# Three PSUM tiles of a decoder trunk draw their banks under another tag

## The chip, the cores and the metric

The kernel runs on one core of a Trainium2 chip. The metric is the device time of one execution in microseconds (us). TensorE (PE in the profile) does the matmuls, VectorE (DVE) and ScalarE (ACT) the elementwise work, GpSimd (POOL) a few small operations, and SP issues the DMAs. Every engine works through its own instructions in the order in which the built program holds them. A matmul writes into PSUM, which this kernel uses as eight banks of 128 x 512 fp32.

## The reference, cut to what is computed

Two layers over 256 tokens of width 1024. Each layer is a half-step FFN, a token mixer, a second half-step FFN and a gated embedding, each closed by a layer norm. The token mixer is where the change lies:

```python
def token_mixing(x, ...):
    h = (x @ w_in).astype(jnp.float32)                # one wide projection
    h_rw, h_gla, h_gdn, h_gate = _split(h, GROUP_SPLITS)
    o_rw = rwkv7_time_mix(h_rw, ...)                  # RWKV-7 recurrence
    o_gla = gla_mix(*_split(h_gla, GLA_SPLITS), ...)  # gated linear attention
    o_gdn = gated_deltanet_mix(*_split(h_gdn, GDN_SPLITS), ...)
    branches = jnp.stack([o_rw, o_gla, o_gdn], axis=2)
    proj = jnp.einsum('btnc,ncd->btnd', branches, w_branch)
    gates = jax.nn.sigmoid(h_gate).reshape(B, T, N_BRANCH, D_MODEL)
    return jnp.sum(gates * proj, axis=2) @ w_o

def gated_deltanet_mix(...):                          # "DeltaNet" below
    q = _l2norm(_heads(q, H, GDN_DK)) * GDN_DK ** -0.5
    k = _l2norm(_heads(k, H, GDN_DK))
    ...
    t_inv = lax.linalg.triangular_solve(eye + lower, ...)   # an inverse per chunk
    ...                                               # then a recurrence over chunks
```

## The kernel before, in words

**Precision.** Every large product is made of three fp32r matmuls: a weight arrives by DMA as `raw` (128 x 1024, one half of a unit), ACT casts it to `hi`, DVE subtracts to get `lo`, and PE runs `hi` with the high part of x (`xh`), `hi` with its low part (`xl`), and `lo` with `xh`.

**Four threads.** Inside a layer's mixer, four Python generators run side by side. S, the stream, makes the blocks of the wide projection: `col_block` fills one PSUM bank, named `cb`, with 48 matmuls of 128 x 256, from two weight halves; then DVE and ACT read the bank (`conv`: one ACT operation and three DVE operations for each 256 columns; `put`: one ACT copy and a DMA to DRAM). R is RWKV (`rwkv`), D is DeltaNet (`gdn`), L is GLA (`gla`). The string `ORDER` says whose next step is recorded. The recorded order is not yet the order on the engines: a scheduler then lists each engine's instructions by priority, and a tile whose pool has no free slot waits for one. So a different pool slot can move instructions on all engines.

**PSUM.** `ps(name, tag)` hands out banks under three tags: A has four banks, F two, G two. `TAGS` overrides the tag by the tile's name. F is what the stream's `cb` blocks rotate through: one bank fills while the other is read out. G is used by the three chains beside it, among others by `lg` (the 64 x 64 products of GLA's eight levels, which take both G banks at once and give them back after a masked copy on DVE), by `rih` and `gih` (the products of the two inverses), `pk`, `gk`, `gks`, `pg` and the transposes `tp`. The rest draws from A.

**The three tiles.** `un` in `unit_norms` is one 128 x 512 matmul that sums squares for the norm of DeltaNet's k and q, four in a layer, each read by an ACT logarithm into `usq`. `ktr` in `gdn` is four transposes in one bank, three times in a layer, read by one ACT copy. `lc` in `gla` is GLA's cross product, two banks in a layer, read by an ACT copy into `lcross`.

**Names in the rows of the mixer.** `rix`, `rih` are RWKV's inverse; `rp`, `ru`, `ry`, `rd` are the matmuls of one of RWKV's four chunk steps, `rpr` and `uz` the copies between them; `pg`, `rv` its output. `pk`, `pq` are DeltaNet's products of k and q; `gig`, `gigt`, `giab` its inverse on DVE; `gix`, `gih`, `gtt`, `gtf`, `gto` its inverse on PE; `gv`, `gd`, `gks`, `go` its recurrence, `gvn`, `gvd`, `grt` the DVE operations between them. `lw` and `latt` are GLA's level weights and its attention, `lo` on PE its output (on DVE, `lo<-raw,hi` is the weight split). `mo`, `var`, `rs` belong to the norm at the end of DeltaNet and GLA. `pj` is the product of a branch with its weights; the first of them needs RWKV's result `bh`, and ends the part in which the threads run side by side.

Of the kernel before, what the change touches and what calls it, by code (L numbers as in the profile page):

```python
# [23 lines left out]
AX = mybir.AxisListType  # L24

RAW, HL, N4, LEAD, FIN = 4, 4, 25, (3, 3), 1
TAGS = {"ab": "A", "gcol": "A", "gih": "G", "gks": "G", "ktr": "F", "lc": "F", "lo": "A", "misc": "G", "pa": "G", "pg": "G", "pj0": "A", "pj1": "A", "pq": "A", "pw": "G", "rih": "G", "st0": "A", "st1": "G", "un": "F"}
PJ = 0
MG = (4, 5)
MO = (3, 3)  # L30
# [204 lines left out]
class Trunk:  # L235
# [66 lines left out]
    def ps(self, name, tag="A"):  # L302

        tag = TAGS.get(name, tag)
        return self.pp.tile([P, 512], F32, tag=tag, name=name, bufs={"A": 4, "F": 2, "G": 2}[tag])
# [1358 lines left out]
```

## Time and profile before

| | us |
|---|---|
| median of 3 runs | 1574.25 (1574.13 to 1577.86) |
| profiled execution, device time | 1568.71 |
| its span, first to last instruction | 1566.9 |
| mean granted TensorE clock | 0.981 |
| mixer of layer 0, first `cb` to first `pj` | 217.0 to 501.4 |
| mixer of layer 1, first `pj` | 1280.3 |

The time of the profiled execution is 1.8 us more than its span, and 5.5 us less than the median. In the profile's tables a row of the view by stages has a stretch of the span, its length, and for each engine the busy time with the count of its instructions; "PEclk" is the clock granted to TensorE as a share of the full one. In the timeline a row has the start, the duration, the engine, the operation with its tiles, the count, and in brackets the idle time of the engine before it and what ended that. In rows of groups the figures behind the bar are the busy time, the mean of one instruction in ns, and the idle time before.

### The profile page before, as it was taken

The numbers are of one execution on the slowest core, as the hardware profiler recorded it, in microseconds if no ns is written. First come the engines' busy times: TensorE is split into PE (matmuls) and PEld (weight loads), VectorE is DVE, ScalarE is ACT, GpSimd is POOL, SyncE is SP. The second block draws the span as 40 slices with busy tenths as digits, with TensorE's granted clock in tenths as the row PEclk, the third lists the DMA queues.
The fourth block names the chain that finished last, engine by engine and source line by source line (L and its number), as shares of the span: only waits on it lengthen the run. The fifth ranks groups of instructions, "written<-read, shape, count | busy, mean of one in ns | idle before, by whom it ended". The sixth has DMA issues, their size and how long they took to land. (4 is left out here: it accounts for less than half of the span.)

```text
span 1566.9 us, 27601 instructions
## 1 busy us (share of the span) xinstructions
PE 1494.9 (95%) x11280; PEld 1356.7 (87%) x11280; DVE 1058.5 (68%) x1597; ACT 873.3 (56%) x1229; POOL 49.1 (3%) x85
## 2 busy tenths in 40 slices
PE   8999999988998999999999999998989889999997
PEld 7999889887987989998789997897979879899986
DVE  5555757787975875556865557577789658745567
ACT  5544558856654554445654445587665555644453
POOL 0000000000002000000000000000000020000001
PEclk9999999989999999999999999999999999999999
DMA  7765655532424655656555666554425256656562
GB/s 257 264 215 189 216 190 161 169 127 80 151 84 168 233 184 177 223 189 216 177 180 192 216 189 194 195 170 153 136 75 156 82 200 219 188 170 222 189 217 81
DMA packets 79775, 277.96 MB, mean 177 GB/s; under 512 B 9376, under 2 KB 9760, under 8 KB 79648
## 3 DMA queue, kind: packets, MB, share of 16 engines
q1 hardware_dynamic: 75744, 262.76, 51.8%
q0 software_dynamic: 3616, 13.11, 2.2%
q8 instruction: 88, 1.44, 0.4%
q10 hardware_dynamic: 288, 0.33, 0.1%
q14 instruction: 39, 0.32, 0.1%
HBM read 264.63 MB, written 11.53 MB: 176 GB/s over the span
## 5 line engine op out<-in xcount | busy, mean ns | idle before, releaser
L223 DVE TENSOR_TENSOR lo<-raw,hi 128x1024 fp32r<-128x1024 f32 (+1 forms) x459 | 555.4, 1220 | 316.1 <-ACT hi L223 313.7
L223 ACT CAST hi<-raw 128x1024 fp32r<-128x1024 f32 (+1 forms) x459 | 474.9, 1047 | 430.1 <-PE h L223 144.1
L223 PE MATMUL h<-xh,hi 128*128 128x256 f32 x1088 | 306.2, 282 | 5.9 <-ACT hi L223 5.5
L223 PE MATMUL h<-xl,hi 128*128 128x256 f32 x1088 | 305.8, 281 | 0.8 <-DVE xl L223 0.8
L223 PE MATMUL h<-xh,lo 128*128 128x256 f32 x1088 | 305.4, 281 | 0.0
L223 PE MATMUL cb<-xh,hi 128*128 128x256 f32 x864 | 247.1, 286 | 14.4 <-DVE c L223 11.1
L223 PE MATMUL cb<-xl,hi 128*128 128x256 f32 x864 | 244.5, 283 | 0.0
L223 PE MATMUL cb<-xh,lo 128*128 128x256 f32 x864 | 243.4, 282 | 0.0
L223 PEld LDWEIGHTS h<-xh,hi 128*128 128x128 f32 x1088 | 204.9, 189 | 7.3 <-ACT hi L223 5.5
L223 PEld LDWEIGHTS h<-xh,lo 128*128 128x128 f32 x1088 | 208.6, 192 | 0.1
L223 PEld LDWEIGHTS h<-xl,hi 128*128 128x128 f32 x1088 | 205.1, 189 | 2.2 <-DVE xl L223 1.0
L223 PEld LDWEIGHTS cb<-xh,hi 128*128 128x128 f32 x864 | 164.7, 191 | 18.8 <-DVE c L223 11.3
L223 PEld LDWEIGHTS cb<-xl,hi 128*128 128x128 f32 x864 | 164.8, 191 | 2.4 <-issue 1.0
L223 PEld LDWEIGHTS cb<-xh,lo 128*128 128x128 f32 x864 | 164.7, 191 | 1.9 <-issue 1.0
L223 PE MATMUL y<-hi,gh 128*128 128x512 f32 x352 | 137.8, 391 | 0.0
L223 PE MATMUL y<-lo,gh 128*128 128x512 f32 x352 | 137.1, 389 | 0.0
L223 PE MATMUL y<-hi,gl 128*128 128x512 f32 x352 | 136.2, 390 | 0.3 <-DVE gl L223 0.3
L223 PE MATMUL tb<-hi,xl 128*128 128x512 f32 x224 | 87.6, 391 | 2.1 <-DVE xl L223 2.1
L223 PE MATMUL tb<-hi,xh 128*128 128x512 f32 x224 | 88.5, 395 | 0.0
L223 PE MATMUL tb<-lo,xh 128*128 128x512 f32 x224 | 88.0, 393 | 0.0
L223 PEld LDWEIGHTS y<-hi,gl 128*128 128x128 f32 x352 | 66.1, 188 | 14.7 <-DVE gl L223 0.8
L223 PEld LDWEIGHTS y<-lo,gh 128*128 128x128 f32 x352 | 66.1, 188 | 12.2
(354 smaller groups left out, 2264.0 us busy)
## 6 DMA issues: line engine op xcount, KB each, us to landing
raw<-in_ws_dram SPq DMA_DIRECT2D x457, 512.0 KB, 4.4
gb<-in_ln_dram SPq DMA_DIRECT2D x16, 512.0 KB, 6.1
gd<-sg SPq DMA_DIRECT2D x32, 256.0 KB, 4.2
sgate<-gd POOLq DMA_DIRECT2D x12, 512.0 KB, 5.8
xd<-x POOLq DMA_DIRECT2D x4, 512.0 KB, 5.8
x<-xd POOLq DMA_DIRECT2D x4, 512.0 KB, 9.0
sw<-in_sw_dram SPq DMA_DIRECT2D x2, 768.0 KB, 8.7
xt<-in_xt_dram SPq DMA_DIRECT2D x4, 256.0 KB, 5.4
```

Of the source, the lines that this page charges most:

```text
L223: ins = f(*args, **kw)
```

## The change

Three entries of the table go from F to G. No instruction is added or removed, and no operation changes; the stream's two banks now serve only the stream, and the two banks of G serve nine more tiles in each layer.

```diff
-TAGS = {"ab": "A", "gcol": "A", "gih": "G", "gks": "G", "ktr": "F", "lc": "F", "lo": "A", "misc": "G", "pa": "G", "pg": "G", "pj0": "A", "pj1": "A", "pq": "A", "pw": "G", "rih": "G", "st0": "A", "st1": "G", "un": "F"}
+TAGS = {"ab": "A", "gcol": "A", "gih": "G", "gks": "G", "ktr": "G", "lc": "G", "lo": "A", "misc": "G", "pa": "G", "pg": "G", "pj0": "A", "pj1": "A", "pq": "A", "pw": "G", "rih": "G", "st0": "A", "st1": "G", "un": "G"}
```

The functions that use the three names:

```python
# unit_norms (DeltaNet's norms)
for sq in sqs:
    for q in range(2):
        ps = self.ps("un", "G")
        self.mm(ps, self.one.to_broadcast([P, P]), sq[:, s])
        nc.scalar.activation(sq[:, s], ps, AF.Ln, bias=self.l2eps)
# gdn
for src, dst in ((kT[:, 0], kt), (v[:, 0], vt[:, 0]), (v[:, 1], vt[:, 1])):
    ps = self.ps("ktr")
    ...
    A.copy(dst, ps.rearrange("p (h c) -> p h c", c=P))
# gla
pss = [self.ps("lc", "G") for _ in range(2)]
```

The scheduler answers with another order. The first place is the norm sums on PE in layer 0, just behind the stream's block that completes DeltaNet's q. Before, on PE:

```order
L223 MATMUL rih<-ritt,riof 64x64 x16
L223 MATMUL rih<-ric,riof 64x64 x16
L223 MATMUL vm<-kc,c_3145 128x128 x3
L223 MATMUL un<-usq,eps 128x512
L223 MATMUL vm<-kc,c_3145 128x128 x5
L223 MATMUL bon<-c_2363,kc 128x512
L223 MATMUL rih<-ric,riof 64x64 x10
L223 MATMUL un<-usq,eps 128x512
L223 MATMUL rih<-ric,riof 64x64 x38
L223 MATMUL un<-usq,eps 128x512 x2
L223 MATMUL pk<-c_2651 128x128 x4
```

Now, on PE at the same place:

```order
L223 MATMUL cb<-xh,lo 128x256
L223 MATMUL un<-usq,eps 128x512 x2
L223 MATMUL vm<-kc,c_3145 128x128 x8
L223 MATMUL bon<-c_2363,kc 128x512
L223 MATMUL cb<-xh,hi 128x256
L223 MATMUL cb<-xl,hi 128x256
```

The two sums for k now come first and together; 82 stream matmuls follow; then come the two sums for q, 20 more stream matmuls, and only then the rest of RWKV's inverse (`rih`), `pq` and `pk`. In all, 102 stream matmuls now stand between `un` and the next `rih`, where none stood.

The second place is DeltaNet's recurrence on PE, late in the mixer. Before, `gd` and `go` stand between blocks of the stream:

```order
L223 MATMUL cb<-xl,hi 128x256
L223 MATMUL cb<-xh,lo 128x256
L223 MATMUL lg<-lw 128x64 x2
L223 MATMUL gd<-gvd,ktst 128x128 x4
L223 MATMUL go<-gvn,dd 128x128 x4
L223 MATMUL lg<-lw 128x64 x6
L223 MATMUL cb<-xh,hi 128x256
```

Now the same instructions on PE follow each other directly:

```order
L223 MATMUL lg<-lw 128x64 x8
L223 MATMUL ry<-ls_2959,vs_3940 64x64
L223 MATMUL lg<-lw 128x64 x4
L223 MATMUL ry<-ls_2961,vs_3940 64x64
L223 MATMUL lg<-lw 128x64 x4
L223 MATMUL ktr<-kc,c_2651 128x128 x4
L223 MATMUL ktr<-kc,c_4418 128x128 x8
L223 MATMUL gv<-vt,giof 128x128 x4
L223 MATMUL lg<-lw 128x64 x8
L223 MATMUL gd<-gvd,ktst 128x128 x4
L223 MATMUL go<-gvn,dd 128x128 x4
```

Of the 1,296 `cb` matmuls of a layer, 1,062 stood ahead of `gix` before and 1,273 stand ahead of it now; behind `gix` 234 were left, and 23 are left now.

The third place is the end of DeltaNet's inverse on DVE, just ahead of `gix`. Now:

```order
L223 TENSOR_TENSOR gigt<-giab 128x225
L223 TENSOR_TENSOR lo<-raw,hi 128x1024
L223 TENSOR_REDUCE giab<-gigt 128x15
L223 TENSOR_TENSOR lo<-raw,hi 128x1024
L223 TENSOR_TENSOR gig<-giab,kc 128x512
L223 STREAM_TRANSPOSE gigt<-gig 128x512
L223 TENSOR_TENSOR gig<-giab,kc 128x512
L223 TENSOR_TENSOR lo<-raw,hi 128x1024
L223 STREAM_TRANSPOSE gigt<-gig 128x512
L223 TENSOR_TENSOR lo<-raw,hi 128x1024 x2
```

From the first copy `rpr<-rp` of RWKV's recurrence to the second of these transposes, DVE held 8 weight splits `lo<-raw,hi` before and holds 13 now, and the 12 `conv` operations of DeltaNet's v (`c_4418`), which were behind the transposes, now stand ahead of them.

## The prediction

> **What bounds the kernel now.** The page comes first: it says which engine sets the time.
>
> ```profile
> span 1566.9 us, 27601 instructions
> PE 1494.9 (95%) x11280; PEld 1356.7 (87%) x11280; DVE 1058.5 (68%) x1597; ACT 873.3 (56%) x1229; POOL 49.1 (3%) x85
> ```
>
> PE is busy for 95% of the span, and the change neither adds nor removes PE work. So only PE's idle time, and the time in which it runs at a lower granted clock, can change. Next comes the view by stages, on the part of layer 0's mixer whose order the change moves: from the `cb` block that completes DeltaNet's q (357.4) over the first `rp` (386.2) and `gix` (418.7) to the first `pj` (501.4); below it the same stages of layer 1.
>
> ```profile
> core 0: us, PE busy (x) PEld busy (x) DVE busy (x) ACT busy (x) POOL busy (x), PEclk, DMA share, GB/s
> 357.40:386.20 28.80, 24.78 (x271) 19.84 (x270) 22.07 (x40) 18.31 (x24) 1.35 (x4) 0.88 0.13 43
> 386.20:418.70 32.50, 32.50 (x337) 30.03 (x336) 30.78 (x68) 20.90 (x31) 0.00 (x0) 1.00 0.52 164
> 418.70:450.00 31.30, 27.58 (x403) 24.39 (x403) 23.94 (x55) 20.28 (x34) 0.52 (x1) 0.89 0.21 68
> 450.00:501.40 51.40, 44.63 (x446) 41.74 (x444) 33.71 (x67) 24.99 (x35) 6.79 (x10) 0.99 0.41 134
> ...
> 1138.10:1165.70 27.60, 23.58 (x271) 18.64 (x270) 21.39 (x39) 18.29 (x24) 1.35 (x4) 0.94 0.13 42
> 1165.70:1198.20 32.50, 32.50 (x337) 30.03 (x336) 31.08 (x69) 20.84 (x31) 0.00 (x0) 1.00 0.52 162
> 1198.20:1229.00 30.80, 26.45 (x404) 23.31 (x404) 24.24 (x55) 20.39 (x34) 0.52 (x1) 0.94 0.23 71
> 1229.00:1280.30 51.30, 44.55 (x445) 41.66 (x444) 33.51 (x67) 24.98 (x35) 5.91 (x8) 0.98 0.41 134
> ```
>
> I call them stages 1 to 4. PE's idle time in layer 0 is 4.02, 0, 3.72 and 6.77, together 14.5. The clock takes 0.12 x 28.8 + 0.11 x 31.3 + 0.01 x 51.4 = 7.4 more. So 144.0 us hold 122.1 of work at full clock and **21.9 of loss**; in layer 1 the same sum gives 15.1 idle and 4.5 of clock, 19.6. Whatever the change does here is the new loss against these two numbers. Who ends the idle time is told by the view of waits for PE in these stages:
>
> ```profile
> PE pj L223 <- ACT bh L223: 6.0, 1, 6.0
> PE un L223 <- ACT usq L223: 4.0, 1, 4.0
> PE gtf L223 <- ACT gt L223: 1.9, 1, 1.9
> PE rv L223 <- ACT rsq L223: 0.8, 1, 0.8
> PE gtt L223 <- DVE giof L223: 0.5, 1, 0.5
> ```
>
> Stage 4 is the one to look at: DeltaNet's recurrence, the last levels of GLA and two RWKV steps run there one behind the other, each waiting for DVE or ACT between two matmuls, and yet PE idles only 0.76 before `rv` and 6.0 before `pj`. What fills the rest is `cb` alone, as the same view restricted to that tile shows:
>
> ```profile
> 386.20:418.70 32.50, 25.34 (x199) 23.34 (x198) 0.00 (x0) 2.84 (x5) 1.00 0.52 164
> 418.70:450.00 31.30, 6.16 (x49) 5.73 (x49) 5.72 (x12) 1.42 (x3) 0.89 0.21 68
> 450.00:501.40 51.40, 23.50 (x188) 21.97 (x186) 0.00 (x0) 2.37 (x4) 0.99 0.41 134
> ```
>
> **Stage 1: the norm sums.** Before, the third `un` stops PE, because ACT, in order, has two table loads, a Silu, an Exp and a square ahead of it.
>
> ```profile
> 371.40 1.22 PE L223 MATMUL un<-usq,eps 128*128 128x512 f32 x1 [4.02 <-ACT usq L223]
> ...
> 366.98 1.06 ACT L223 ACTIVATE c<-c 128x1024 f32<-128x1024 f32 x1
> 368.06 1.28 ACT L223 ACT_TABLE_LOAD   x1
> 369.35 1.06 ACT L223 ACTIVATE usq<-usq 128x1024 f32<-128x1024 f32 x1
> 370.31 1.04 ACT L223 ACTIVATE usq<-c 128x1024 f32<-128x1024 f32 x1
> ```
>
> Now 82 `cb` matmuls stand in that gap. They need weights: the next two halves are cast at 356.1 and 357.4 and last for 48 matmuls, but the casts for the second 48 stand behind ACT's Silu of q, which waits for DVE's last `conv`, and that for the Exp of k ahead of it on DVE. Walking down the new order with these durations, I get: `un` from 357.4, `vm`, `bon`, 48 `cb` to 368.4; Silu 368.3, first cast done 370.4, its `lo` on DVE 371.6. So PE idles some 3.0 (with two matmuls between) before the remaining 34, and about 1.7 more where q's Ln and Exp hold the next casts. The first `rp` then ends near 392.0 instead of 386.9, with 63 more `cb` done. A `cb` matmul goes every 0.12 us (25.34 for 199, less the overlap of their ends), so those are worth 7.5. **Net 2.4 less in a layer.** Bounds: 7.5 less, if no cast is late and the clock stays up (4.02 + 3.46); 1 more, if these waits lower the clock as the old one did.
>
> **Stage 2: the fill runs ahead.** 346 `cb` now stand between there and `gix`, 41.5 of PE; `gk`, `ru`, `ry`, `rd`, `lg` and the rest of the stage are 9 (32.5 less 198 x 0.12). PE needs 50.5. But DVE held 30.78 in 32.50 here. It now gets 5 more `lo`, 12 `conv`, one more pair of `latt`, and the start of the inverse (`at`, `dd`, `gig`, 7.0 between 379.96 and 387.6, since `pk` comes later):
>
> ```profile
> L223 DVE TENSOR_TENSOR lo<-raw,hi 128x1024 fp32r<-128x1024 f32 x457 | 554.1, 1222 | 315.9 <-ACT hi L223 313.4 <-issue 0.3 <-PE cb L223 0.3
> L223 DVE SCALAR_TENSOR_TENSOR c<-cb,cv,c 128x255 f32<-128x255 f32 x48 | 22.6, 477 | 4.1 <-ACT c L223 3.7
> L223 DVE COPY_PREDICATED latt<-masks,lg 128x256 f32<-128x256 uint8 x28 | 13.1, 526 | 4.4 <-PE lg L223 4.4
> ...
> 379.96 1.13 DVE L223 SCALAR_TENSOR_TENSOR at<-pk,nb,dd 128x128 f32<-128x128 f32 x4 [0.42 <-PE pk L223]
> 387.53 0.68 DVE L223 TENSOR_TENSOR c<-c,erke 128x512 f32<-128x512 f32 x1
> ```
>
> 30.8 + 5 x 1.22 + 12 x 0.48 + 2 x 0.53 + 7.0 = 50.7: DVE and PE are now equally long, and each block of 48 needs its second `lo` after only 12 matmuls. The walk finds PE waiting for `lo` four times: 1.3 and 2.8 where the start of GLA's levels stands before it on DVE, 2.0 behind an `lg` group, 1.2 at the inverse's end. **7 more in a layer**, bounds 0 (DVE runs ahead, as it did) and 12 (DVE starts as late as its 6.7 of idle time in stage 1 allow, on top of half of that in order waits). `gix` then starts near 450 where its 211 extra `cb` and one `lg` group (25.3 + 1.1) would put it at 445: 5 behind, stages 1 and 2 together.
>
> **Stages 3 and 4: the uncovered tail.** 82.7 before, less these 26.4 that are done already: even at 56.3. PE's work there at full clock is 82.7 - 10.5 - 4.0 - 26.4 = 41.8 (10.5 idle and 4.0 of clock, from the stages above). Walking the new order from `gix` = 0 with the rows' durations:
>
> ```profile
> 438.78 1.09 PE L223 MATMUL gtt<-kc,giof 128*128 128x128 f32 x8 [0.52 <-DVE giof L223]
> 441.81 0.45 PE L223 MATMUL gtf<-gt,at 128*64 128x64 f32 x8 [1.93 <-ACT gt L223]
> 501.41 0.79 PE L223 MATMUL pj<-bh,hi 128*128 128x256 f32 x2 [6.02 <-ACT bh L223]
> ...
> 458.39 1.23 DVE L223 TENSOR_TENSOR dgate<-dgate,br 128x1024 f32<-128x1024 f32 x1 [0.55 <-DMA dgate<-gd]
> 463.08 0.70 DVE L223 TENSOR_TENSOR gvd<-gvn,ec 128x512 f32<-128x512 f32 x1
> 470.71 1.12 DVE L223 SCALAR_TENSOR_TENSOR mo<-go,rs,dgate 128x128 f32<-128x128 f32 x4 [1.18 <-POOL rs L445]
> ```
>
> `gtt` waits 1.4 for `giof` and `gtf` 0.8; `rd` 1.3 and `ry` 1.0 for the copies of RWKV's state; `ktr` 0.7, because in G it must wait until DVE has emptied the banks of two `lg` groups; `gv` runs at 30; `gd` waits 2.4, since the multiply of `dgate` (1.23) stands between `gvn` and `gvd` on DVE; the transposes `tp` wait 1.5 for the norm over POOL, and `gks` stands behind them on PE and the second `gv` behind that; RWKV's last `ru` comes at 46, `rv` at 51, and the 7.8 from `rv` to `pj` (6.0 of them idle) stay. `pj` at 59.5: **3 more in a layer** than even. Bounds: 48.5, 8 less, if only the wait before `pj` stays; 11 more, if two drops of the clock (3.4 each, below) come on top of waits that are 4 longer.
>
> **The clock.** Finer stages show what a gap costs behind it:
>
> ```profile
> 371.40:374.80 3.40, 3.40 (x4) 1.51 (x5) 2.92 (x6) 2.44 (x4) 0.00 (x0) 0.50 0.00 0
> 440.00:443.40 3.40, 1.15 (x20) 1.01 (x22) 1.82 (x5) 2.02 (x4) 0.00 (x0) 0.82 0.00 0
> 443.40:450.00 6.60, 6.37 (x91) 5.67 (x89) 5.28 (x13) 4.60 (x10) 0.00 (x0) 0.57 0.01 2
> ```
>
> After 4.02 idle the granted clock is 0.50; and it is 0.57 after a stretch in which the longest single gap was 1.93, so a run of short gaps is enough. The walk's gaps in stages 1, 3 and 4 are of that kind. I count no drop beyond those at `pj`, which stays, because the places can't be told; one drop costs at most 3.4, two 6.8.
>
> The Trainium skill ("TensorE: Matmul & The Clock Gate", Part 1: The HAM clock gate) lets the clock fall to half only after a whole idle window of about 3.4 us. The 0.57 above, behind gaps of at most 1.93, speaks against that reading. By the rule none of the walk's gaps would drop it, and the sum is the one I take; by the rows it would be 3 to 7 more in a layer.
>
> **The sum.** -2.4 + 7 + 3 = 7.6, say 8 in a layer and 16 in two (layer 1 has the same order here but for a few rows, and 2 less to lose from its clock). The profiled execution took 1568.7, 1.8 outside its span: 1568.7 + 16 = 1584.7. The median of the runs lies 5.5 higher, and the new time will be such a median: **1590**.
>
> **Rivals.** (a) *The fill simply does its work earlier*: stage 1 gives back the full 7.5, DVE keeps up in stage 2, and the tail's waits lie under each other's matmuls, costing 1. That is 6.5 less in a layer, 1561. For it speaks that the old gap at `un` is real and PE bound all of stage 2 without a gap; against it that DVE had 1.7 of slack in 32.5 there. It decides where the new loss from 357.4 to `pj` falls under 21.9 in layer 0; the walk has 4.7 + 7.3 + 17.7 = 29.7 before any clock. (b) *The waits only change places*: the saved 7.4 of stage 1 equals the new waits, within 4.7 of 1574. It needs a quarter less waiting than the walk has. (c) *G jams*: `lg`, `gih`, `pg`, `tp` and now `ktr` and `lc` hold two banks in turn; if each of the nine tiles waits 0.6 for a bank, 5, and the clock falls once, 3.4, on top of the 7.6, it is 16 in a layer, 1606. That the change is empty can't be: the order above differs.
>
> **How the numbers follow.** A measurement of this kernel can tell 0.3%, 4.7 us, from no change. Slower by more, forecast and (c), 0.68 (0.53 and 0.15); within, (b), 0.13; faster by more, (a), 0.19. The range goes from 1564, most of the way to (a), to (c) at 1606. The single bounds, all added at one end, would reach further, but they exclude each other: what DVE is late in stage 2 it need not do in the tail.
>
> **What would show it.** Right: `un` without its 4.0; PE idle in stage 2 ended by DVE `lo`; between `gix` and `pj` no `cb` but a few, and idle time before `gd`, `tp`, `rd`, 15 or more. Wrong: stage 2 without gaps, a `gix` to `pj` under 53, or PE idle in the mixer no more than before. What would make it wrong most easily is the walk itself: it takes every copy as late as its engine's order allows, and one release that comes earlier shortens all behind it.

## The result, and the profile after

| | before | after |
|---|---|---|
| median of the runs, us | 1574.19 (1571.76 to 1577.86, 4 runs) | 1595.56 (1594.83 to 1596.31, 4 runs) |
| span of the profiled execution, us | 1566.9 | 1593.1 |
| mean granted TensorE clock | 0.981 | 0.975 |
| layer 0, first `cb` to first `pj`, us | 284.4 | 297.1 |
| layer 1, the same, us | 284.6 | 297.7 |

The changed kernel takes **1.0134 times as long, 95% interval 1.0118 to 1.0149**: 21.4 us more in the medians, 26.2 us more between the two profiled executions, since the one of before lay 5.5 below its median. One execution of `all_to_a`, a kernel of the experiments below, ran at a mean clock of 0.844 and took 1650.5 us; its ratio leaves that one out. The two mixers hold 12.7 + 13.1 = 25.8 of these 26.2. The page's first lines already say what kind of time it is:

```profile
span 1593.1 us, 27610 instructions
PE 1506.5 (95%) x11280; PEld 1366.7 (86%) x11280; DVE 1059.0 (66%) x1597; ACT 871.8 (55%) x1229; POOL 51.8 (3%) x85
```

The same 11,280 matmuls took 11.6 us more of busy time, and the mean granted clock fell from 0.981 to 0.975, so part of them ran at a lower clock; the other 14.6 of the 26.2 are idle. The view by stages shows where. The rows are stage 1, stage 2 and stages 3 and 4 together, of layer 0 and then of layer 1. Here layer 0 begins 0.8 later (217.8 instead of 217.0), and stage 1 begins at 358.0 instead of 357.4.

```profile
core 0: us, PE busy (x) PEld busy (x) DVE busy (x) ACT busy (x) POOL busy (x), PEclk, DMA share, GB/s
358.00:393.30 35.30, 31.50 (x342) 26.36 (x341) 21.62 (x32) 22.75 (x30) 0.44 (x2) 0.95 0.35 110
393.30:444.50 51.20, 50.10 (x491) 47.83 (x490) 47.42 (x107) 28.96 (x40) 0.00 (x0) 1.00 0.43 140
444.50:515.00 70.50, 53.77 (x625) 47.19 (x625) 42.77 (x95) 32.10 (x53) 9.60 (x13) 0.85 0.20 65
1152.70:1185.90 33.20, 29.37 (x333) 25.01 (x333) 21.05 (x30) 22.75 (x30) 0.44 (x2) 1.00 0.37 117
1185.90:1237.70 51.80, 50.56 (x501) 48.19 (x500) 47.92 (x108) 28.91 (x40) 0.00 (x0) 1.00 0.44 133
1237.70:1306.70 69.00, 53.56 (x625) 46.95 (x625) 42.78 (x95) 32.08 (x53) 8.72 (x11) 0.85 0.21 70
```

Read idle time as the length less PE's busy time, and the clock's loss as the length times what PEclk lacks of 1. In stage 2 PE idles 1.1 in 51.2, at full clock. Behind `gix` (third and sixth row) it idles 16.7 and 15.4, and the clock takes 0.15 x 70.5 = 10.6 and 10.4 more. Before, that part had 10.5 and 4.0 in layer 0. The same view for `cb` alone shows what is gone there:

```profile
358.00:393.30 35.30, 14.76 (x114) 0.95 0.35 110
393.30:444.50 51.20, 42.48 (x346) 1.00 0.43 140
444.50:515.00 70.50, 3.42 (x23) 0.85 0.20 65
```

23 stream matmuls are left behind `gix`, where there were 234. The longest waits of PE from 358 to 515 follow: who waits, for whom, total us, times, longest.

```profile
PE tp L223 <- DVE mo L223: 8.7, 2, 7.1
PE gd L223 <- DVE gvd L223: 2.1, 1, 2.1
PE pq L223 <- DVE c L223: 1.8, 1, 1.8
PE gtt L223 <- DVE giof L223: 1.7, 1, 1.7
PE cb L223 <- DVE c L223: 1.3, 2, 0.7
PE rih L223 <- ACT usq L223: 1.1, 1, 1.1
PE gtf L223 <- ACT gt L223: 1.0, 1, 1.0
PE ry L223 <- ACT vs L223: 0.8, 1, 0.8
```

The 4.0 before `un` is gone. No wait for DVE's `lo` shows. The long wait at the end, which was 6.0 at `pj` before, belongs to `tp` now, since five of these transposes stand ahead of the first `pj`. Finer stages of the tail show the clock:

```profile
459.90:463.40 3.50, 1.52 (x16) 1.17 (x16) 1.57 (x5) 3.25 (x6) 0.00 (x0) 1.00 0.62 191
463.40:470.20 6.80, 5.88 (x94) 5.31 (x94) 5.91 (x15) 3.13 (x7) 0.00 (x0) 0.50 0.00 0
470.20:473.60 3.40, 2.42 (x36) 2.11 (x36) 2.82 (x8) 0.81 (x2) 0.31 (x1) 1.00 0.02 5
473.60:480.40 6.80, 6.80 (x31) 5.91 (x31) 3.22 (x9) 1.97 (x4) 0.54 (x1) 0.50 0.21 75
480.40:483.90 3.50, 1.89 (x23) 1.59 (x21) 3.27 (x7) 0.84 (x2) 0.00 (x0) 0.99 0.01 4
483.90:487.30 3.40, 2.88 (x13) 2.88 (x14) 1.67 (x3) 0.59 (x1) 0.00 (x0) 0.50 0.01 2
```

Three times a stretch of 3.4 at full clock, of which PE idled 1.0 to 2.0, in gaps that are each at most the 2.1 before `gd`, is followed by half clock, for 6.8, 6.8 and 3.4. A fourth drop, 0.50 from 511.2, comes behind the wait at `tp`. But not each such stretch has one: from 490.7 to 494.1 PE idled 1.1 of 3.4, and the next 3.4 ran at 1.00.

### The profile page after: what moved, and what is told of

Same layout as the page of the kernel before. It is cut to its first block, busy times and chain, and to the rows that moved or that the text cites. A ratio compares the mean times of both kernels' runs of the same rounds, so it can differ in the third digit from the quotient of the medians.

```text
span 1593.1 us, 27610 instructions
## 1 busy us (share of the span) xinstructions
PE 1506.5 (95%) x11280; PEld 1366.7 (86%) x11280; DVE 1059.0 (66%) x1597; ACT 871.8 (55%) x1229; POOL 51.8 (3%) x85
## 5 line engine op out<-in xcount | busy, mean ns | idle before, releaser
L223 PEld LDWEIGHTS y<-hi,gl 128*128 128x128 f32 x352 | 66.1, 188 | 14.2 <-DVE gl L223 0.4
```

The lines of the kernel that those rows point to most:

```text
L223: ins = f(*args, **kw)
```

## The experiments

Each kernel is compared with the kernel before, run beside it on the same chip; the first four of the experiments, the next four and the last four ran on three different chips. Two numbers from each trace go with the time: when the last matmul of the second `pk` starts, and when the first `pj` starts, both counted from the layer's first `cb` (layer 0 / layer 1). They stand in one table, with PE's idle time and the clock's loss between the first `cb` and the first `pj`, worked out from the view by stages as above (cut at the first `un`, the first `rp` and `gix`). Length less both losses, PE's work at full clock, comes to 246 to 251 in most rows and 241 to 254 at the extremes, as it should: no kernel but `warm_tail` (257) adds work. A second decimal of PEclk that is rounded moves a loss by up to 0.7 in a stretch of 140, so small differences mean nothing. The row of after is against a median of 1574.19 for before, the others against the 1575.43, 1575.62 and 1575.09 of the three chips.

| kernel | median, us | ratio, 95% interval | second `pk` | first `pj` | idle | clock |
|---|---|---|---|---|---|---|
| before | 1575.1 to 1575.6 | 1 | 162.6 / 163.5 | 284.4 / 284.6 | 23.3 / 25.6 | 13.2 / 10.0 |
| after | 1595.56 | 1.0134 (1.0118 to 1.0149) | 178.5 / 180.4 | 297.1 / 297.7 | 30.7 / 31.0 | 17.8 / 17.6 |
| un_only | 1610.96 | 1.0232 (1.0200 to 1.0264) | 177.2 / 181.1 | 303.7 / 302.9 | 38.7 / 39.3 | 24.0 / 19.6 |
| un_ktr | 1599.49 | 1.0164 (1.0136 to 1.0193) | 177.9 / 178.8 | 298.2 / 298.6 | 32.0 / 32.7 | 20.2 / 18.7 |
| ktr_only | 1576.92 | 1.0014 (0.9997 to 1.0030) | 162.2 / 162.5 | 283.6 / 284.0 | 24.7 / 25.9 | 5.4 / 9.1 |
| lc_only | 1574.10 | 0.9994 (0.9983 to 1.0005) | 162.4 / 163.1 | 287.0 / 287.1 | 24.6 / 26.0 | 12.6 / 11.8 |
| ktr_lc | 1578.16 | 1.0008 (0.9994 to 1.0023) | 162.9 / 164.7 | 286.5 / 285.8 | 22.4 / 23.1 | 12.5 / 9.8 |
| un_to_a | 1580.18 | 1.0021 (1.0006 to 1.0036) | 161.3 / 162.1 | 285.9 / 288.1 | 25.3 / 26.3 | 14.3 / 16.5 |
| all_to_a | 1571.27 | 0.9969 (0.9954 to 0.9984) | 161.9 / 162.6 | 282.5 / 284.1 | 23.3 / 23.6 | 11.7 / 13.7 |
| warm_tail | 1592.94 | 1.0090 (1.0074 to 1.0107) | 179.0 / 180.0 | 294.4 / 293.9 | 25.8 / 27.6 | 11.2 / 9.3 |
| pk_free | 1583.14 | 1.0059 (1.0038 to 1.0080) | 152.7 / 155.3 | 289.7 / 291.9 | 26.6 / 29.3 | 14.2 / 12.6 |
| pk_half | 1601.18 | 1.0158 (1.0134 to 1.0181) | 169.3 / 172.1 | 294.8 / 296.7 | 31.8 / 34.0 | 16.6 / 15.2 |
| un_a_rest_g | 1588.87 | 1.0089 (1.0071 to 1.0106) | 161.1 / 161.3 | 292.2 / 290.7 | 26.8 / 27.9 | 16.6 / 12.3 |
| all_a_pk_free | 1575.89 | 1.0005 (0.9994 to 1.0016) | 156.9 / 156.0 | 285.4 / 285.3 | 24.3 / 26.2 | 11.7 / 9.9 |

### One entry at a time

The first question is which of the three tiles does it. Each of these is the kernel before with only the entries shown changed.

```diff
-"un": "F"
+"un": "G"     (un_only)
```

> Only the norm sums un go to G; ktr and lc stay with the stream's banks. Theory cover (what costs time is how much of the stream is left to fill the chains' waits behind gix): 1,104 cb stand ahead of gix in layer 0, 192 remain behind it, spread between gv, gd and gks as before, so the tail keeps its cover and the wait of 4.0 us before the third un goes: 1560 to 1572 us, ratio 0.991 to 0.999. Rival jam (G's two banks are short, and every tile moved there waits for one): four of the nine tiles of a layer move, so four ninths of the 21 us: about 1584 us, ratio 1.006. If the stage 1 part of the prediction holds alone (2.4 less in a layer), 1569 us.

```diff
-"ktr": "F"
+"ktr": "G"    (ktr_only)
```

> Only the transposes ktr go to G; un and lc stay. Theory cover: gix stands where it stood (1,062 cb ahead) but at gv, gd and gks 1,248 are done instead of 1,152 to 1,248, 48 remain, and the old wait before un stays at 4.0: slower, 1580 to 1596 us, ratio 1.004 to 1.014, with new idle time on PE before gtf, gd and tp. Rival jam: three of nine tiles, 1581 us, ratio 1.004, with the idle time before ktr and lg.

```diff
-"lc": "F"
+"lc": "G"     (lc_only)
```

> Only GLA's cross product lc goes to G. Theory cover: the stream stands as before but for 28 matmuls between lc and the second gv: no change, 1571 to 1577 us, ratio 0.998 to 1.002. Rival jam: two of nine tiles, 1579 us, ratio 1.003, with idle time before lc or lg.

```diff
-"ktr": "F", "un": "F"
+"ktr": "G", "un": "G"    (un_ktr)
```

> un and ktr go to G, lc stays. Theory cover: 1,248 cb stand ahead of gix (1,273 with the whole change), 48 remain behind it: nearly the whole loss, 1588 to 1596 us, ratio 1.009 to 1.014. The two parts do not add: un alone gains and ktr alone loses less. Rival jam: seven of nine tiles, 1591 us, and it is the sum of the two parts alone.

`un` alone costs 36 us, more than all three together; `ktr` alone and `lc` alone cannot be told from no change, though both theories had `ktr` at 1580 or more, and the theory jam had `lc` at 1579; `un` with `ktr` costs 24, more than either theory had. So the change's cost comes in with `un`, and `ktr` in G takes a part of it back. Neither theory foresaw 1611 for `un_only`. Its stages in layer 0 (from the first `rp`, with a cut where the stream stops and where it goes on), and the middle one of them for `cb` alone:

```profile
389.60:421.70 32.10, 32.10 (x362) 30.02 (x361) 29.12 (x68) 16.21 (x24) 0.00 (x0) 1.00 0.37 115
421.70:470.60 48.90, 30.35 (x371) 27.01 (x370) 29.59 (x71) 20.53 (x34) 0.52 (x1) 0.65 0.07 23
470.60:522.00 51.40, 44.49 (x435) 41.58 (x434) 33.12 (x65) 25.09 (x35) 7.82 (x10) 0.97 0.41 134
```

```profile
421.70:470.60 48.90, 0.02 (x1) 0.65 0.07 23
```

And what PE waited for in the middle row:

```profile
PE ktr L223 <- ACT c L223: 5.3, 1, 5.3
PE lg L223 <- DVE lw L223: 5.2, 1, 5.2
PE gtt L223 <- DVE giof L223: 4.3, 1, 4.3
PE gix L223 <- ACT git L223: 2.2, 1, 2.2
```

From 421.7 to 470.6 not one stream matmul runs: `ktr` is still in F there, and the stream's next block starts at 470.6, behind the last `ktr` at 464.6. PE idles 18.5 of 48.9 and has a clock of 0.65. Moving `ktr` too (un_ktr, after) opens this wall; the stream then runs on, and is used up by `gix`. Either way the same loss arises: a stretch in which only the chains run, and PE waits for DVE and ACT between their matmuls.

Why `un` should lead there is told by `pk`. These are its rows in the trace, before, then in `un_only`, then in the changed kernel (durations of one, first and last start):

```profile
L223 PE MATMUL pk<-c x16: 273/348/422, 375.0 to 379.6; 128*128 128x128 f32 x16
```

```profile
L223 PE MATMUL pk<-c x16: 271/275/378, 390.9 to 395.5; 128*128 128x128 f32 x16
```

```profile
L223 PE MATMUL pk<-c x16: 270/275/377, 391.7 to 396.3; 128*128 128x128 f32 x16
```

`pk`, the start of DeltaNet's inverse, runs 15 to 16 us later, counted from the layer's first `cb`, though it computes the same from the same k. Before, `un` in F stopped the stream as well as PE, and `pk` came right behind it. In the order that the scheduler makes with `un` in G, the second pair of `un` (for q) needs ACT's work on q, and `rih` and `pk`, which draw from G behind it, come after it, while the stream, no longer stopped, puts its matmuls ahead: 946 instead of 832 of the layer's `cb` stand ahead of the second `pk`. In all four kernels that have `un` and `pk` in G (after, un_only, un_ktr, warm_tail), `pk` is late by 15 to 18 us; in those with `un` in F it isn't.

### Is it the bare tail, or the late start of DeltaNet?

```diff
-"ktr": "F", "lc": "F"
+"ktr": "G", "lc": "G"    (ktr_lc)
```

> un stays with the stream's banks, ktr and lc go to G. Theory chain (DeltaNet's chain from pk over its inverse and recurrence to pj sets the end of the mixer, 117 to 126 us from the second pk to the first pj in all six kernels run so far, so what counts is how early pk runs on PE; un in G puts 102 cb ahead of it): pk stands where it stood, 162 to 163 us behind the layer's first cb, so pj comes 280 to 287 us behind it (284.5 before): 1566 to 1580 us, ratio 0.995 to 1.003, though only 38 cb are left behind the first ktr. Rival cover (the tail loses its fill): that tail is as bare as with the whole change, 1588 to 1597 us, ratio 1.009 to 1.014.

```diff
-"un": "F"
+"un": "A"     (un_to_a)
```

> un leaves the stream's banks for the class of four banks (A) instead of G; ktr and lc stay. In the order RWKV's inverse rih and pk no longer stand behind the second pair of un: 42 cb ahead of pk instead of 16, and nothing waits 4.0 us for the square of q. Theory chain: the second pk runs 3 to 4 us earlier than before in a layer: 1564 to 1571 us, ratio 0.993 to 0.998. Rival (taking un out of the stream's banks costs time wherever it goes, since the stream then runs ahead and meets ktr's banks too early, as in the run with un alone in G): 1590 us or more.

```diff
-"ktr": "F", "lc": "F", "un": "F"
+"ktr": "A", "lc": "A", "un": "A"    (all_to_a)
```

> All three tiles leave the stream's banks, as in the change, but for A instead of G. Theory chain: pk as early as with un alone in A, 3 to 4 us earlier than before, and a bare tail costs nothing by itself: 1560 to 1571 us, ratio 0.990 to 0.998. Theory cover: 84 cb are left behind the first ktr instead of 192: slower, 1580 to 1590 us, ratio 1.004 to 1.010.

`ktr_lc` moves the two other tiles just as the change does, and costs nothing that can be measured, as the theory chain expected: with `pk` early, its tail loses 9.5 idle and 3.4 of clock in layer 0, no more than before's 10.5 and 4.1. So with `un` in F the two tiles in G aren't a cost. `all_to_a` takes all three out of the stream's banks, which is what the change does, but into A's four banks: `pk` stays early, PE idles 1.7 instead of 4.0 between the first `un` and the first `rp`, and the kernel is **faster than before, by 0.31% (0.16 to 0.46)**, the only one that is, and at the edge of the 0.3% that the prediction called measurable. `un_to_a` missed both of its forecasts: `pk` is as early, yet it comes out 0.2% slower, inside what I had called no change. Its clock loses 8.7 and 9.6 behind `gix`, where before loses 4.1 and 2.5; why the clock falls there more often was not followed up.

### The clock by itself

`warm_tail` is the changed kernel with matmuls that only keep PE at work: 16 ahead of `gtt` and 16 ahead of `gd` in each layer (each of them is two matmul records in the profile), into banks that the next matmuls write anew.

```diff
         for t in range(NT):
             ps = self.ps("gtt")
+            for m in range(8):
+                self.mm(ps[:, m % 4 * P:m % 4 * P + P], self.ident, f8(at)[:, m])
...
                 pd = h3(self.ps("gd"))
+                for m in range(16):
+                    self.mm(pd[:, m % 4], kt[:, m % 4], vn[:, m % 4])
```

> The whole change, with 16 extra matmuls of 128 x 128 ahead of gtt and 16 ahead of gd in each layer, written to the same bank and overwritten by the real ones; they fill part of the two longest waits of the tail so that TensorE's granted clock falls less often. They add 8 us of PE work in all, meant to lie in idle time. Theory clock (the 17 us at half clock per layer in the tail make the tail long): half-clock time between gix and pj falls to 10 us or less in a layer, 1587 to 1592 us against 1595.6 with the change. Theory chain: the waits for DVE and ACT set the tail, whose matmuls on the chain are few: 1593 to 1599 us.

The row of its tail in layer 0, from `gix` to `pj`:

```profile
445.60:512.70 67.10, 55.00 (x683) 49.57 (x683) 41.46 (x91) 32.34 (x53) 7.27 (x11) 0.94 0.21 68
```

Idle 12.1 instead of 16.7, clock 0.06 x 67.1 = 4.0 instead of 10.6: 11 of loss less, for 8 more of work that does nothing, so the tail is 3.4 shorter; the median is 2.6 us less (4.0 less if each is taken over the kernel before beside it). At 1592.94 it lies between the two forecasts, so the median decides for neither; the trace shows that the half clock is real time and shrinks when the gaps are filled: PE's useful work went through sooner, although more was put ahead of it. But gaps filled with work that does nothing gain little.

### `pk` taken out of the queue

The last four test the late `pk` directly. The first two are the changed kernel with one entry more.

```diff
+"pk": "F"     (pk_free)
```

> The changed kernel with one entry more in TAGS: pk (DeltaNet's k by k product) in F, so that it no longer stands behind un and rih in G's two banks. un, ktr and lc stay in G. In the new order 816 cb matmuls stand ahead of both pk (946 ahead of the second one in the changed kernel, 832 in the one before). Theory chain (what costs is that pk runs late, since DeltaNet's chain from the second pk to the first pj takes 117 to 126 us in every kernel): second pk 160 to 165 us after the first cb of the layer, first pj 281 to 290 after it, time 1566 to 1582, about that of the kernel before. Theory jam (three more tiles in G's two banks cost by themselves): they are all still there, time stays at 1590 to 1600. Theory clock (half clock in the bare tail behind gix): ktr and lc stay late, and the drops with them, 1585 to 1596.

```diff
+"pk": "A"     (pk_half)
```

> The changed kernel with pk in A's four banks instead of G. The new order has 909 cb matmuls ahead of the second pk, between the 832 of before and the 946 of the changed kernel; 1158 stand ahead of gix. Theory chain: a dose between, the time goes with the place of pk; 77 of the 114 cb that the change put ahead of it remain, so about two thirds of 21 us: 1586 to 1592, second pk 171 to 177 us after the layer's first cb. Theory jam: one tile fewer in G, so a share of what pk cost there at most: 1590 to 1597.

```diff
-"un": "G"
+"un": "A"     (un_a_rest_g, against the changed kernel)
```

> The changed kernel with un in A's four banks, ktr and lc in G. 858 cb stand ahead of the second pk, as in all_to_a and un_to_a. Theory chain: second pk 161 to 163 us after the layer's first cb, first pj 282 to 288, time 1568 to 1578; the 1580 of un_to_a then came from ktr and lc in F, where they stop the stream. Theory jam: ktr and lc in G wait for banks that A would give, 1578 to 1586.

```diff
-"ktr": "F", "lc": "F", "un": "F"
+"ktr": "A", "lc": "A", "pk": "F", "un": "A"    (all_a_pk_free, against the kernel before)
```

> un, ktr and lc in A as in all_to_a, and pk in F besides: 816 cb ahead of both pk instead of 858, 1062 ahead of gix instead of 1104. Theory chain, if nothing else holds pj by then: 42 cb of 0.12 us less ahead of pk, 5 us in a layer: 1558 to 1566. Rival (with pk this early it is PE's own work that sets the place of pj, no longer the chain): as all_to_a, 1567 to 1575.

`pk_free` lies just over the 1582 of its forecast. It gives back 12.4 of the 21.4 us (13.3, if each is taken over the kernel before beside it) with nothing changed but the bank of `pk`, and so the order that the scheduler makes: `pk` starts at 366.2 instead of 391.7.

```profile
L223 PE MATMUL pk<-c x16: 421/421/579, 366.2 to 370.9; 128*128 128x128 f32 x16
```

Its stages of layer 0:

```profile
358.40:391.30 32.90, 27.21 (x270) 21.61 (x268) 21.73 (x40) 19.21 (x26) 1.34 (x4) 0.79 0.11 36
391.30:423.50 32.20, 31.91 (x336) 29.56 (x335) 29.94 (x66) 18.87 (x27) 0.00 (x0) 1.00 0.52 164
423.50:507.90 84.40, 72.40 (x853) 66.47 (x853) 60.64 (x127) 46.25 (x71) 9.56 (x13) 0.98 0.34 108
```

The tail is covered again: 12.0 idle and 1.7 of clock instead of 16.7 and 10.6. Much of what it still loses against before is in stage 1, 5.7 and 6.9 against 4.0 and 3.4, where `pk` now stands so early that PE waits for its input:

```profile
PE pk L223 <- DVE c L223: 4.3, 2, 3.3
PE un L223 <- ACT usq L223: 1.4, 1, 1.4
```

But the theory as I had put it, that the way from `pk` to `pj` takes 117 to 126 whatever the kernel, fell with the same run: here it takes 137. `all_a_pk_free` says it again: with `pk` another 5 us earlier than in `all_to_a`, `pj` comes no earlier and the median isn't lower. So a `pk` that is earlier than before gains nothing. That PE's own work then sets `pj`, as the rival had it, fits but is not shown, since PE still idles 24 to 26 in each of these mixers.

The first `pj` also needs RWKV's result, and RWKV's recurrence starts later in the changed kernel as well: the first `rp` comes 172.6 behind layer 0's first `cb`, where it came 169.2 behind it before. This alone does not cost it: in `pk_free` it comes at 173.1 and in `all_a_pk_free` at 176.2, and yet the one gains and the other is as fast as the kernel before.

`un_a_rest_g` has `pk` as early as `all_to_a`, and was forecast at 1568 to 1578, or 1578 to 1586 by the theory jam; it took 1588.9. So an early `pk` gives back only 6.7 of the 21.4 us here. Up to `gix` it is like `all_to_a` within 2 us; behind it, in layer 0, it needs 85.3 where the other needs 75.5. PE's waits there, in this kernel and then in `all_to_a`:

```profile
PE tp L223 <- DVE mo L223: 9.5, 2, 7.1
PE gih L223 <- ACT gitt L223: 1.7, 1, 1.7
```

```profile
PE pj L223 <- ACT bh L223: 5.5, 1, 5.5
PE gih L223 <- ACT gitt L223: 2.2, 1, 2.2
```

With `ktr` and `lc` in G, the transposes `tp` wait 2.4 for the norm in the middle of the recurrence, and five of them stand ahead of the first `pj` and hold it for 7.1, as in the changed kernel; in `all_to_a` `pj` waits 5.5 itself. Its idle time there comes to 3.6 more than in `all_to_a`, and its clock takes 4.2 more (0.12 of 85.3 against 0.08 of 75.5). So the two tiles do cost in G here, 8 to 10 us behind `gix`, while in `ktr_lc`, where `un` is in F, they cost nothing measurable. What makes the difference between these two settings was not tried.

`pk_half` answers to neither theory (1586 to 1592 and 1590 to 1597 were forecast, 1601.2 was measured). It shows that `pk` leaving G isn't enough by itself: from A it runs only 8 to 9 us earlier than in the changed kernel. Its mixers are 2.3 and 1.0 shorter than the changed kernel's, which has the sign that the earlier `pk` should give. Part of what the earlier `pk` should bring is spent ahead of `gix`: in both layers `cb` waits there once for DVE's `c`, for 5.9, where the longest such wait in the changed kernel's stage 2 is 0.5. Its median is 5.6 higher all the same. In its profiled execution the stretch from the first `pj` of layer 0 to the first `cb` of layer 1 takes 501.6, where the changed kernel takes 494.1 and others lie between. No run here shows why, and it stays open.

## Why the prediction came out right, and which of its steps did not

The forecast of 1590, slower, held: 1595.56 lies in the range. Its own steps fared as follows.

- **Stage 1, -2.4: the size right, the waits others.** The first `rp` was to end 34.6 behind the start of the stage; it ended 35.3 behind it. `un` no longer waits, and new waits took part of the gain. But the walk had 3.0 and 1.7 in the stream, for late weights; measured are 1.8 at `pq` and 0.7 at `cb`, for DVE's `c`, and 1.1 at `rih`.
- **Stage 2, +7: wrong.** It was to take 58 from there to `gix`, with PE waiting four times for `lo`. It took 51.2, 1.1 of that idle, and no wait for `lo` shows: the lower bound of 0. The step that failed is "DVE and PE are now equally long". They nearly are (DVE was busy for 47.4 of 51.2, where the sum had 50.7), but the walk took every copy as late as its engine's order allowed, and DVE came in time instead. The upper bound of 12 isn't the sum of its terms: 6.7 and half of it make 10.
- **Stages 3 and 4, +3: the sum of the waits right, the clock wrong.** The walk had 17.7 of waits and 41.8 of work; measured are 16.7 and 70.5 - 16.7 - 10.6 = 43.2. What was mis-sized is the clock: "I count no drop beyond those at `pj`", and it took 10.6 and 10.4 in the two layers. The term is 70.4 less the even 56.3, **+14**. The bound "11 more" counts from the walk's 59.5 (4 of longer waits and two drops of 3.4), while "8 less" counts from the even 56.3; put on one footing the upper bound is 14 above even, just what was measured. But it came about otherwise: the waits were 1 shorter, not 4 longer, and the clock took 10.6, not 6.8, in four drops.
- **The clock's rule.** The sum had counted no new drop. The Trainium skill ("TensorE: Matmul & The Clock Gate", Part 1: The HAM clock gate) has the half clock come after at least one idle window of about 3.4 us. The rows quoted in the prediction had spoken against that as a condition, and they were right: the finer stages above show half clock behind 3.4 us of which PE idled only 1.0. By those rows, 3 to 7 more in a layer, the forecast would have been 1596 to 1604, and the lower end is what was measured.
- **The sum.** An error of 7 too much and one of 11 too little left 12.7 and 13.1 in a layer for the forecast 8. The direction rested on the uncovered tail and did hold; the nearness of the number is partly luck. Of the prediction's own signs, those in the tail came (no `cb` but 23, and 16.7 idle, most of it at `tp`, `gd` and `gtt`), the idle time in stage 2 that `lo` ends did not, and a sign of being wrong, stage 2 without gaps, came but for 1.1 us.
- **The rivals.** (a), work done earlier, had the stage without a gap that it needed, and lost in the tail. (b) is excluded by the interval. (c), G jams, named a right thing, G's two banks, but not the way in which it acts: what shows is not each tile waiting 0.6 for a bank, but `pk` standing behind `un` and `rih`, which moved the start of a chain by 16 us.

What stood in the orders and was weighed too lightly is that last point. The prediction wrote "since `pk` comes later", and used it only as a load for DVE in stage 2. The two kernels that bring `pk` forward by 17 to 26 us give back 12.4 (by the bank of `pk`) and 6.7 (by the bank of `un`) of the 21.4 us, so the late `pk` is a part of the cost, of about that size. A third, `pk_half`, brings it forward by 8 to 9 and gives back nothing. The rest is not assigned: freeing `pk` adds waits of its own in stage 1, and `un_a_rest_g` shows that `ktr` and `lc` in G can cost too.

## What to carry to other kernels

When tiles move from one set of banks to another, look first for what else draws from the new set behind them, and how early that stands on its engine; a start that comes later spends the work that was to cover the waits at the end. Count a bare stretch twice: by its waits, and by the half clock behind them (16.7 and 10.6 us here). And ask whether a larger set will do: here freeing the stream's banks gained 0.3%, at the edge of what can be told, with A's four banks, and lost 1.3% with G's two.

## What the runs showed of the hardware that was not expected

The granted clock can fall to half behind a stretch that is mostly busy: in the changed kernel behind 3.4 us with 1.0 idle (470.2 to 473.6) as well as behind 3.5 with 2.0 idle (459.9 to 463.4). It does not always: behind 3.4 us with 1.1 idle (490.7 to 494.1) it stayed at 1.00, so the idle share alone does not decide, and what does is open. Once fallen, it stays at half for one or two such stretches, even where PE idles for no moment of them (6.80 busy of 6.80 from 473.6). In the stage without `cb` of `un_only`, 18.5 idle of 48.9, it is 0.65 on the mean. Matmuls put into the gaps brought the tail's mean from 0.85 to 0.94.
